# Row softmax on one core: row maxima moved to a general path, five large tiles in place of ten, late loads between two loops

## The chip, the cores and the metric

One core of a Trainium2 chip. The time is the device's, in microseconds (us), from one execution; the "span" of a profile, from its first to its last instruction, is 1.3 to 1.4 us shorter. On this one core "slow" means a run over 1.5% above the fastest of its kernel.

## The reference, cut to what matters

```python
x: (16, 1024, 512) float32
x_scaled = x / 2.0
exp_x = np.exp(x_scaled - np.max(x_scaled, axis=-1, keepdims=True))
return exp_x / np.sum(exp_x, axis=-1, keepdims=True)
```

There are 16384 rows of 512 numbers. On the chip they lie as 128 partitions by 128 rows; "a row" below is one row on all 128 partitions: 0.262 MB. All data are read once and written once, 67.1 MB in all.

## The kernel before

It keeps 98 rows on chip (the arena). Ten tiles of 3 to 15 rows are loaded, worked on in place and stored; the last two reuse the places of the first four. VectorE finds row maxima, ScalarE computes exp with its row sum, VectorE divides. SyncE issues the stores, ScalarE nearly all loads.

```python
PLAN = [
    ([3], 0), ([4, 3], 3), ([5, 4, 4], 10), ([5] * 3, 23), ([5] * 3, 38), ([5] * 3, 53),
    ([5] * 3, 68), ([5] * 3, 83), ([5] * 3, 0), ([5] * 3, 15),
]                                        # rows of each chunk of a tile, place in the arena
LAG = 2
...
    def do_max(k):
        nc.vector.reduce_max(out=stats[:, b : b + c], in_=arena[:, a : a + c], negate=True, ...
        )._wait_ge(ld[t], ...).then_inc(s_max, 1)
...
        for k in range(len(chunks) + LAG):
            if k < len(chunks):
                do_max(k)
            if k >= LAG:
                do_mul(k - LAG)          # reciprocal of the sums, then the product
...
                ins = nc.scalar.activation(
                    out=arena[:, a + r], in_=arena[:, a + r], func=Exp, scale=0.5,
                    bias=stats[:, b + r : b + r + 1], accum_out=stats[:, b + r : b + r + 1],
                )
...
        for t in range(len(tiles)):      # SyncE
            nc.sync.wait_ge(s_mul, last_chunk[t] + 1)
            nc.sync.dma_start(out=dram(of, t), in_=sb(t)).then_inc(...)
```

Of the kernel before, what the change touches and what calls it, by code (L numbers as in the profile page):

```python
# [6 lines left out]




PLAN = [
    ([3], 0), ([4, 3], 3), ([5, 4, 4], 10), ([5] * 3, 23), ([5] * 3, 38), ([5] * 3, 53),
    ([5] * 3, 68), ([5] * 3, 83), ([5] * 3, 0), ([5] * 3, 15),
]
ARENA = 98
LAG = 2

SPREAD = 1

AFTER = {8: 4, 9: 5}  # L20

FUSED = {1, 2, 3}

LOOP = 6
E = 5


@with_exitstack
def kernel(
# [5 lines left out]
    nc = tc.nc  # L35
    tc.close()
    tc.compile()
    fp32 = mybir.dt.float32

    xf = x.flatten_outer_dims()  # L40
    of = out.flatten_outer_dims()
    N, D = xf.shape
    P = nc.NUM_PARTITIONS
    n_rows = N // P
    assert sum(sum(c) for c, _ in PLAN) == n_rows

    arena = nc.alloc_sbuf_tensor("arena", (P, ARENA, D), fp32)

    stats = nc.alloc_sbuf_tensor("stats", (P, n_rows), fp32)
    recip = nc.alloc_sbuf_tensor("recip", (P, n_rows), fp32)  # L50



    tiles, chunks, base = [], [], 0
    for t, (cs, at) in enumerate(PLAN):
        r = sum(cs)
        tiles.append((base, r, at))
        o = 0
        for c in cs:
            chunks.append((t, base + o, c, at + o))  # L60
            o += c
        base += r
    last_chunk = {c[0]: k for k, c in enumerate(chunks)}

    def dram(ap, t):
        b, r, _ = tiles[t]
        return ap[b * P : (b + r) * P].rearrange("(p r) d -> p r d", r=r)

    def sb(t):
        _, r, at = tiles[t]  # L70
        return arena[:, at : at + r, :]


    behind = {}
    for t, (_, r, at) in enumerate(tiles):
        for u in range(t):
            _, ru, au = tiles[u]
            if at < au + ru and au < at + r:
                behind.setdefault(t, []).append(u)

    ld = [nc.alloc_semaphore(f"ld{t}") for t in range(len(tiles))]
    awaited = sorted({u for us in behind.values() for u in us})


    st, need = {}, {}
    for t in sorted(behind):
        new = [u for u in behind[t] if u not in st]
        sem = nc.alloc_semaphore(f"st{t}")
        st.update({u: sem for u in new})
        need[t] = (sem, 16 * len(new))  # L90
    s_end = nc.alloc_semaphore("s_end")
    s_max = nc.alloc_semaphore("s_max")
    s_exp = nc.alloc_semaphore("s_exp")
    s_go = nc.alloc_semaphore("s_go")
    s_rec = nc.alloc_semaphore("s_rec")
    s_mul = nc.alloc_semaphore("s_mul")

    def issue_loads(begin, end):


        for t in range(begin, end):
            if t in behind:
                continue
            if t == 0:
                nc.sync.dma_start(out=sb(t), in_=dram(xf, t)).then_inc(ld[t], 16)
            elif t == SPREAD:

                r = tiles[t][1] - 1
                for p, q, lo, hi in ((0, P, 0, r), (0, 126, r, r + 1), (126, P, r, r + 1)):
                    nc.scalar.dma_start(  # L110
                        out=sb(t)[p:q, lo:hi], in_=dram(xf, t)[p:q, lo:hi]
                    ).then_inc(ld[t], 16)
            else:
                nc.scalar.dma_start(out=sb(t), in_=dram(xf, t)).then_inc(ld[t], 16)

    def do_max(k):
        t, b, c, a = chunks[k]
        nc.vector.reduce_max(  # L118
            out=stats[:, b : b + c],
            in_=arena[:, a : a + c],  # L120
            axis=mybir.AxisListType.X,
            negate=True,
        )._wait_ge(ld[t], 48 if t == SPREAD else 16).then_inc(s_max, 1)

    def do_mul(k):
        t, b, c, a = chunks[k]
        nc.vector.reciprocal(  # L127
            out=recip[:, b : b + c], in_=stats[:, b : b + c]
        )._wait_ge(s_exp, k + 1).then_inc(s_rec, 1)
        if t in FUSED:  # L130
            nc.vector.tensor_mul(  # L131
                out=arena[:, a : a + c],
                in0=arena[:, a : a + c],
                in1=recip[:, b : b + c].unsqueeze(2).to_broadcast([P, c, D]),
            )._wait_ge(s_rec, k + 1).then_inc(s_mul, 1)
            return
        for r in range(c):
            ins = nc.vector.tensor_scalar_mul(  # L138
                out=arena[:, a + r],
                in0=arena[:, a + r],  # L140
                scalar1=recip[:, b + r : b + r + 1],
            )
            if r == 0:
                ins._wait_ge(s_rec, k + 1)
        ins.then_inc(s_mul, 1)

    def compute_and_store():

        for k in range(len(chunks) + LAG):
            if k < len(chunks):  # L150
                do_max(k)
            if k >= LAG:
                do_mul(k - LAG)


        for t in range(len(tiles)):
            nc.sync.wait_ge(s_mul, last_chunk[t] + 1)
            nc.sync.dma_start(out=dram(of, t), in_=sb(t)).then_inc(
                st[t] if t in awaited else s_end, 16
            )  # L160

        nc.sync.wait_ge(s_end, 16 * (len(tiles) - len(awaited)))


        straight = [k for k, c in enumerate(chunks) if c[0] < LOOP]
        loop = [k for k, c in enumerate(chunks) if c[0] >= LOOP]
        for k in loop:
            nc.tensor.wait_ge(s_max, k + 1).then_inc(s_go, 1)


        nc.scalar.preload_act_table(mybir.ActivationFunctionType.Exp)  # L171
        late = sorted(behind)
        for k in straight:
            t, b, c, a = chunks[k]
            for r in range(c):
                ins = nc.scalar.activation(  # L176
                    out=arena[:, a + r],
                    in_=arena[:, a + r],
                    func=mybir.ActivationFunctionType.Exp,
                    bias=stats[:, b + r : b + r + 1],  # L180
                    scale=0.5,
                    accum_out=stats[:, b + r : b + r + 1],
                )
                if r == 0:
                    ins._wait_ge(s_max, k + 1)
            ins.then_inc(s_exp, 1)
            while late and last_chunk[AFTER[late[0]]] <= k:
                u = late.pop(0)
                nc.scalar.wait_ge(*need[u])
                nc.scalar.dma_start(out=sb(u), in_=dram(xf, u)).then_inc(ld[u], 16)  # L190
        assert not late


        first = chunks[loop[0]][1]
        assert all(
            c == E and b == first + j * E and a == b % ARENA
            for j, (_, b, c, a) in enumerate(chunks[k] for k in loop)
        )
        row = nc.scalar.alloc_register("row")
        nc.scalar.reg_mov(row, first)  # L200
        with nc.scalar.While(lambda: nc.scalar.snap(row, min_val=first, max_val=n_rows) < n_rows):
            now = nc.scalar.snap(row, min_val=first, max_val=n_rows - E)
            nc.scalar.wait_ge(s_go, 1).then_inc(s_go, -1)  # L203
            at = nc.s_assert_within(
                now % ARENA, 0, ARENA - E,
                skip_runtime_bounds_check_because="no chunk reaches over the arena's end",
            )
            for r in range(E):
                data = arena[:, r : ARENA - E + 1 + r][:, bass.ds(at, 1)]
                stat = stats[:, r : n_rows - E + 1 + r][:, bass.ds(now, 1)]  # L210
                ins = nc.scalar.activation(  # L211
                    out=data,
                    in_=data,
                    func=mybir.ActivationFunctionType.Exp,
                    bias=stat,
                    scale=0.5,
                    accum_out=stat,
                )
            ins.then_inc(s_exp, 1)
            nc.scalar.reg_add(row, row, E)  # L220



    here = str(nc.cur_bb)
    entry, rest = nc.main_func.blocks[0], list(nc.main_func.blocks[1:])
    head, jumps = entry.instructions[:-5], entry.instructions[-5:]
    entry.instructions = []
    nc.switch_bb("main", None)
    issue_loads(0, 2)
    first = list(entry.instructions)  # L230
    at = next(k for k, i in enumerate(head) if type(i).__name__ == "InstDrain")
    entry.instructions = head[:at] + first + head[at:]
    act = []
    entry.instructions = list(entry.instructions) + [i for i in jumps if i not in act]
    nc.switch_body(here, parent=None, valid_engines=[i.engine for i in jumps])
    issue_loads(2, len(tiles))
    compute_and_store()


# [28 lines left out]
```

## Time and profile before

| | before |
|---|---|
| time | 160.08 us, median of 3 |
| span of the profile | 158.6 us |
| VectorE busy | 131.4 us |
| ScalarE busy | 94.4 us |
| bytes over the span | 67.1 MB, 423 GB/s |

The prediction shows the lines of the profile. In them DVE is VectorE, ACT ScalarE, PE TensorE, POOL GpSimd and SP SyncE; a q after a name is the queue on which that engine issues, and L132 is a line of the kernel. Two things to keep in mind when reading them: the DMA row says in how many tenths of each slice the 16 DMA engines moved something, and it is full nearly everywhere; and a row of idle time on VectorE or ScalarE costs nothing while that is so.

### The profile page before, as it was taken

What the parts mean: (1) busy time and instruction counts of PE and PEld (TensorE: products, weight loads), DVE (VectorE), ACT (ScalarE), POOL (GpSimd) and SP (SyncE); (2) the same over time, 40 slices, a digit from 0 to 9 for tenths busy, and PEclk for the clock granted to TensorE, in tenths of its full rate; (3) what the DMA queues carried; (4) which work ended last, traced back from release to release, by engine and by line L of the source; (5) the groups of instructions that cost most, each with busy time, mean ns of one, the idle gap of its engine ahead of it and who ended that gap; (6) DMA issues with size and microseconds to landing.
All of it is one profiled execution on the core that took longest, in us unless ns stands there. A gap on an engine that the chain in (4) does not pass through costs nothing.

```text
span 158.6 us, 621 instructions
## 1 busy us (share of the span) xinstructions
DVE 131.4 (83%) x155; ACT 94.4 (60%) x257; POOL 0.2 (0%) x4
## 2 busy tenths in 40 slices
DVE  0466799999999999999999999996999389999000
ACT  0369197736874594669738797666566809763000
POOL 0000000000000000000000000000000000000000
DMA  7999999999999999999999999999999999999996
GB/s 268 449 373 430 414 431 466 435 407 399 466 443 389 434 463 448 418 444 426 442 426 434 426 426 442 426 441 411 457 395 472 395 473 395 472 395 465 395 472 263
DMA packets 3026, 67.13 MB, mean 423 GB/s; under 512 B 336, under 2 KB 336, under 8 KB 720
## 3 DMA queue, kind: packets, MB, share of 16 engines
q1 hardware_dynamic: 1584, 34.34, 50.6%
q10 hardware_dynamic: 1440, 32.77, 48.5%
q14 instruction: 2, 0.02, 0.0%
HBM read 33.55 MB, written 33.55 MB: 423 GB/s over the span
## 4 chain that ended last, share of the span: by engine, by line
DMA 52%; DVE 38%; issue 0%
DMA arena<-in_x_dram 38%; DVE stats L118 18%; DMA out_dram<-arena 14%; DVE arena L131 13%; DVE arena L138 7%; DVE recip L127 1%
## 5 line engine op out<-in xcount | busy, mean ns | idle before, releaser
L118 DVE TENSOR_REDUCE stats<-arena 128x5 f32<-128x2560 f32 (+2 forms) x27 | 72.2, 2676 | 14.6 <-DMA arena<-in_x_dram 14.6
L176 ACT ACTIVATE arena<-arena,stats 128x512 f32<-128x512 f32 x68 | 48.2, 710 | 23.4 <-DVE stats L118 23.4
L211 ACT ACTIVATE arena<-arena,stats x60 | 42.5, 710 | 20.7 <-ACTq L203 20.7
L138 DVE TENSOR_SCALAR arena<-arena,recip 128x512 f32<-128x512 f32 x93 | 38.6, 482 | 0.7
L131 DVE TENSOR_TENSOR arena<-arena,recip 128x2560 f32<-128x2560 f32 (+2 forms) x8 | 19.9, 2491 | 0.3
L176 ACT ACTIVATION_READ_ACCUMULATOR arena<-arena,stats 128x1 f32 x68 | 12.7, 187 | 0.0
L211 ACT ACTIVATION_READ_ACCUMULATOR arena<-arena,stats x60 | 11.2, 187 | 0.0
L127 DVE RECIPROCAL recip<-stats 128x5 f32<-128x5 f32 (+2 forms) x27 | 4.8, 177 | 0.0
L171 ACT ACT_TABLE_LOAD x1 | 1.3, 1283 | 5.7 <-issue 5.7
L252 POOL MEMSET const-bfloat16-1.0<- 128x1 bf16 x1 | 0.1, 101 | 0.0
L252 POOL MEMSET const-uint8-127<- 128x1 uint8 x1 | 0.1, 101 | 0.0
L252 POOL MEMSET const-float32-0.0<- 128x1 f32 x1 | 0.1, 98 | 0.2 <-issue 0.2
L252 POOL MEMSET const-float32-1.0<- 128x1 f32 x1 | 0.1, 98 | 0.0
## 6 DMA issues: line engine op xcount, KB each, us to landing
arena<-in_x_dram ACTq DMA_DIRECT2D x7, 3840.0 KB, 46.6
out_dram<-arena SPq DMA_DIRECT2D x7, 3840.0 KB, 22.7
arena<-in_x_dram ACTq DMA_DIRECT2D x1, 3328.0 KB, 14.3
out_dram<-arena SPq DMA_DIRECT2D x1, 3328.0 KB, 21.1
out_dram<-arena SPq DMA_DIRECT2D x1, 1792.0 KB, 18.2
arena<-in_x_dram ACTq DMA_DIRECT2D x1, 1536.0 KB
arena<-in_x_dram SPq DMA_DIRECT2D x1, 768.0 KB, 6.2
out_dram<-arena SPq DMA_DIRECT2D x1, 768.0 KB, 15.8
```

The lines of the kernel that those rows point to most:

```text
L118: nc.vector.reduce_max(out=stats[:, b : b + c], in_=arena[:, a : a + c], axis=mybir.AxisListType.X, negate=True,)._wait_ge(ld[t], 48 if t ...
L127: nc.vector.reciprocal(out=recip[:, b : b + c], in_=stats[:, b : b + c])._wait_ge(s_exp, k + 1).then_inc(s_rec, 1)
L131: nc.vector.tensor_mul(out=arena[:, a : a + c], in0=arena[:, a : a + c], in1=recip[:, b : b + c].unsqueeze(2).to_broadcast([P, c, D]),)._w ...
L138: ins = nc.vector.tensor_scalar_mul(out=arena[:, a + r], in0=arena[:, a + r], scalar1=recip[:, b + r : b + r + 1],)
L171: nc.scalar.preload_act_table(mybir.ActivationFunctionType.Exp)
L176: ins = nc.scalar.activation(out=arena[:, a + r], in_=arena[:, a + r], func=mybir.ActivationFunctionType.Exp, bias=stats[:, b + r : b + r ...
L211: ins = nc.scalar.activation(out=data, in_=data, func=mybir.ActivationFunctionType.Exp, bias=stat, scale=0.5, accum_out=stat,)
L252: nc = _bacc.Bacc("TRN2", target_bir_lowering=False, num_devices=1)
```

## The change

The intent: VectorE, the busiest engine, is freed of the row maxima. exp(x/2) is taken without subtracting anything; at the end the kernel counts the row sums that lie between 1 and 1e30, and only if one doesn't, a general path computes everything again with maxima. The ten tiles become five. Two loads that reuse the arena are issued by ScalarE between two loops, after row 70.

```diff
-PLAN = [ ([3], 0), ([4, 3], 3), ([5, 4, 4], 10), ([5] * 3, 23), ... ]
+TILES = [(30, 8), (30, 38), (30, 68), (25, 0), (13, 25)]     # rows, place
+TURN = 70
...
-                do_max(k)
...
-                    bias=stats[:, b + r : b + r + 1],
...
+    def early():
+        load(nc.sync, 0)
+    def loads():
+        load(nc.scalar, 1)
+        load(nc.scalar, 2)
...
+        exponentials(0, TURN)
+        nc.scalar.wait_ge(s_first, 16)        # store of tile 0 has landed
+        load(nc.scalar, 3)
+        load(nc.scalar, 4)
+        exponentials(TURN, n_rows - LAST)
...
+        nc.vector.tensor_scalar(out=inside, in0=stats, scalar1=LO, scalar2=HI, op0=max, op1=min)
+        ... is_equal, reduce_sum, a 1x1 matmul, flag
+        rounds(nc.vector, vector); rounds(nc.scalar, scalar); rounds(nc.sync, sync)   # general path
```

(Shortened; cut are semaphores, asserts and the general path's body. All 26 products are now one tensor_mul per chunk of five rows, three in the last.)

More of the change, by code (lines that the diff above doesn't have):

```diff
@@ L6 @@
 from concourse._compat import with_exitstack
-PLAN = [
-    ([3], 0), ([4, 3], 3), ([5, 4, 4], 10), ([5] * 3, 23), ([5] * 3, 38), ([5] * 3, 53),
-    ([5] * 3, 68), ([5] * 3, 83), ([5] * 3, 0), ([5] * 3, 15),
-]
+TILES = [(30, 8), (30, 38), (30, 68), (25, 0), (13, 25)]
 ARENA = 98
-LAG = 2
-SPREAD = 1
-AFTER = {8: 4, 9: 5}
-FUSED = {1, 2, 3}
-LOOP = 6
+SHIFT = 8
 E = 5
+LAST = 3
+TURN = 70
+LO, HI = 1.0, 1.0e30
+G = 8
 @with_exitstack
@@ L38 @@
     fp32 = mybir.dt.float32
+    Exp = mybir.ActivationFunctionType.Exp
+    Alu = mybir.AluOpType
     xf = x.flatten_outer_dims()
@@ L44 @@
     n_rows = N // P
-    assert sum(sum(c) for c, _ in PLAN) == n_rows
+    assert sum(r for r, _ in TILES) == n_rows
     arena = nc.alloc_sbuf_tensor("arena", (P, ARENA, D), fp32)
@@ L50 @@
     recip = nc.alloc_sbuf_tensor("recip", (P, n_rows), fp32)
-    tiles, chunks, base = [], [], 0
-    for t, (cs, at) in enumerate(PLAN):
-        r = sum(cs)
+    inside = nc.alloc_sbuf_tensor("inside", (P, n_rows), fp32)
+    count = nc.alloc_sbuf_tensor("count", (P, 1), fp32)
+    ones = nc.alloc_sbuf_tensor("ones", (P, 1), fp32)
+    flag = nc.alloc_sbuf_tensor("flag", (1, 1), mybir.dt.int32)
+    g_max = nc.alloc_sbuf_tensor("g_max", (P, G), fp32)
+    g_sum = nc.alloc_sbuf_tensor("g_sum", (P, G), fp32)
+    total = nc.alloc_psum_tensor("total", (1, 1), fp32)
+    tiles, base = [], 0
+    for r, at in TILES:
+        assert at == (base + SHIFT) % ARENA
         tiles.append((base, r, at))
-        o = 0
-        for c in cs:
-            chunks.append((t, base + o, c, at + o))
-            o += c
         base += r
-    last_chunk = {c[0]: k for k, c in enumerate(chunks)}
     def dram(ap, t):
@@ L71, in sb @@
         return arena[:, at : at + r, :]
-    behind = {}
-    for t, (_, r, at) in enumerate(tiles):
-        for u in range(t):
-            _, ru, au = tiles[u]
-            if at < au + ru and au < at + r:
-                behind.setdefault(t, []).append(u)
-    ld = [nc.alloc_semaphore(f"ld{t}") for t in range(len(tiles))]
-    awaited = sorted({u for us in behind.values() for u in us})
-    st, need = {}, {}
-    for t in sorted(behind):
-        new = [u for u in behind[t] if u not in st]
-        sem = nc.alloc_semaphore(f"st{t}")
-        st.update({u: sem for u in new})
-        need[t] = (sem, 16 * len(new))
+    starts = list(range(0, n_rows - LAST, E)) + [n_rows - LAST]
+    sizes = [E] * (len(starts) - 1) + [LAST]
+    assert n_rows - LAST == E * (len(starts) - 1)
+    owner = [max(t for t, (b, _, _) in enumerate(tiles) if b <= s) for s in starts]
+    assert all(s + c <= sum(tiles[t][:2]) for s, c, t in zip(starts, sizes, owner))
+    upto = [1 + max(k for k, o in enumerate(owner) if o == t) for t in range(len(tiles))]
+    ld = [nc.alloc_semaphore(f"ld{t}") for t in range(len(tiles))]
+    s_first = nc.alloc_semaphore("s_first")
     s_end = nc.alloc_semaphore("s_end")
-    s_max = nc.alloc_semaphore("s_max")
     s_exp = nc.alloc_semaphore("s_exp")
@@ L96 @@
     s_mul = nc.alloc_semaphore("s_mul")
-    def issue_loads(begin, end):
-        for t in range(begin, end):
-            if t in behind:
-                continue
-            if t == 0:
-                nc.sync.dma_start(out=sb(t), in_=dram(xf, t)).then_inc(ld[t], 16)
-            elif t == SPREAD:
-                r = tiles[t][1] - 1
-                for p, q, lo, hi in ((0, P, 0, r), (0, 126, r, r + 1), (126, P, r, r + 1)):
-                    nc.scalar.dma_start(
-                        out=sb(t)[p:q, lo:hi], in_=dram(xf, t)[p:q, lo:hi]
-                    ).then_inc(ld[t], 16)
-            else:
-                nc.scalar.dma_start(out=sb(t), in_=dram(xf, t)).then_inc(ld[t], 16)
@@ L116, in do_max @@
-    def do_max(k):
-        t, b, c, a = chunks[k]
-        nc.vector.reduce_max(
-            out=stats[:, b : b + c],
-            in_=arena[:, a : a + c],
-            axis=mybir.AxisListType.X,
-            negate=True,
-        )._wait_ge(ld[t], 48 if t == SPREAD else 16).then_inc(s_max, 1)
-    def do_mul(k):
-        t, b, c, a = chunks[k]
-        nc.vector.reciprocal(
-            out=recip[:, b : b + c], in_=stats[:, b : b + c]
-        )._wait_ge(s_exp, k + 1).then_inc(s_rec, 1)
-        if t in FUSED:
+    s_ones = nc.alloc_semaphore("s_ones")
@@ new lines, with load, store @@
+    s_cnt = nc.alloc_semaphore("s_cnt")
+    s_tot = nc.alloc_semaphore("s_tot")
+    s_flag = nc.alloc_semaphore("s_flag")
+    g_ld = nc.alloc_semaphore("g_ld")
+    g_st = nc.alloc_semaphore("g_st")
+    g_neg = nc.alloc_semaphore("g_neg")
+    g_exp = nc.alloc_semaphore("g_exp")
+    g_rec = nc.alloc_semaphore("g_rec")
+    g_mul = nc.alloc_semaphore("g_mul")
+    def load(eng, t):
+        eng.dma_start(out=sb(t), in_=dram(xf, t)).then_inc(ld[t], 16)
+    def store(t):
+        nc.sync.wait_ge(s_mul, upto[t])
+        nc.sync.dma_start(out=dram(of, t), in_=sb(t)).then_inc(
+            s_first if t == 0 else s_end, 16
+        )
@@ new lines, in take, with rounds @@
+    def take(eng, sem, n):
+        eng.wait_ge(sem, n).then_inc(sem, -n)
+    def rounds(eng, body):
+        last = n_rows // G
+        i = eng.alloc_register("tile")
+        eng.wait_ge(s_flag, 1)
+        eng.reg_load(i, flag[0:1, 0:1])
+        with eng.While(lambda: eng.snap(i, min_val=0, max_val=last) < last):
+            body(eng.snap(i, min_val=0, max_val=last - 1))
+            eng.reg_add(i, i, 1)
+    def early():
[3 more added lines that the diff above has]
+        load(nc.scalar, 2)
@@ L131, in do_mul, with program @@
+    def program():
+        nc.vector.memset(ones[:, :], 1.0).then_inc(s_ones, 1)
+        for k, (b, c) in enumerate(zip(starts, sizes)):
+            a = (b + SHIFT) % ARENA
+            nc.vector.reciprocal(
+                out=recip[:, b : b + c], in_=stats[:, b : b + c]
+            )._wait_ge(s_exp, k + 1).then_inc(s_rec, 1)
             nc.vector.tensor_mul(
@@ L135, in do_mul @@
             )._wait_ge(s_rec, k + 1).then_inc(s_mul, 1)
-            return
-        for r in range(c):
-            ins = nc.vector.tensor_scalar_mul(
-                out=arena[:, a + r],
-                in0=arena[:, a + r],
-                scalar1=recip[:, b + r : b + r + 1],
-            )
-            if r == 0:
-                ins._wait_ge(s_rec, k + 1)
-        ins.then_inc(s_mul, 1)
-    def compute_and_store():
-        for k in range(len(chunks) + LAG):
-            if k < len(chunks):
-                do_max(k)
-            if k >= LAG:
-                do_mul(k - LAG)
-        for t in range(len(tiles)):
-            nc.sync.wait_ge(s_mul, last_chunk[t] + 1)
-            nc.sync.dma_start(out=dram(of, t), in_=sb(t)).then_inc(
-                st[t] if t in awaited else s_end, 16
-            )
-        nc.sync.wait_ge(s_end, 16 * (len(tiles) - len(awaited)))
-        straight = [k for k, c in enumerate(chunks) if c[0] < LOOP]
-        loop = [k for k, c in enumerate(chunks) if c[0] >= LOOP]
-        for k in loop:
-            nc.tensor.wait_ge(s_max, k + 1).then_inc(s_go, 1)
-        nc.scalar.preload_act_table(mybir.ActivationFunctionType.Exp)
-        late = sorted(behind)
-        for k in straight:
-            t, b, c, a = chunks[k]
-            for r in range(c):
-                ins = nc.scalar.activation(
-                    out=arena[:, a + r],
-                    in_=arena[:, a + r],
-                    func=mybir.ActivationFunctionType.Exp,
-                    bias=stats[:, b + r : b + r + 1],
-                    scale=0.5,
-                    accum_out=stats[:, b + r : b + r + 1],
-                )
-                if r == 0:
-                    ins._wait_ge(s_max, k + 1)
-            ins.then_inc(s_exp, 1)
-            while late and last_chunk[AFTER[late[0]]] <= k:
-                u = late.pop(0)
-                nc.scalar.wait_ge(*need[u])
-                nc.scalar.dma_start(out=sb(u), in_=dram(xf, u)).then_inc(ld[u], 16)
-        assert not late
-        first = chunks[loop[0]][1]
-        assert all(
-            c == E and b == first + j * E and a == b % ARENA
-            for j, (_, b, c, a) in enumerate(chunks[k] for k in loop)
-        )
-        row = nc.scalar.alloc_register("row")
@@ new lines, in program @@
+        nc.vector.tensor_scalar(
+            out=inside[:, :], in0=stats[:, :], scalar1=LO, scalar2=HI,
+            op0=Alu.max, op1=Alu.min,
+        ).then_inc(s_cnt, 1)
+        nc.vector.tensor_tensor(
+            out=inside[:, :], in0=inside[:, :], in1=stats[:, :], op=Alu.is_equal
+        )._wait_ge(s_cnt, 1).then_inc(s_cnt, 1)
+        nc.vector.reduce_sum(
+            out=count[:, :], in_=inside[:, :], axis=mybir.AxisListType.X
+        )._wait_ge(s_cnt, 2).then_inc(s_cnt, 1)
+        nc.vector.tensor_scalar(
+            out=flag[:, :], in0=total[:, :], scalar1=float(N), scalar2=float(n_rows // G),
+            op0=Alu.is_ge, op1=Alu.mult,
+        )._wait_ge(s_tot, 1).then_inc(s_flag, 1)
@@ new lines, in program @@
+        for t in range(len(tiles)):
+            nc.tensor.wait_ge(ld[t], 16).then_inc(s_go, owner.count(t))
+        nc.tensor.wait_ge(s_ones, 1)
+        nc.tensor.matmul(
+            total[:, :], lhsT=count[:, :], rhs=ones[:, :], start=True, stop=True
+        )._wait_ge(s_cnt, 3).then_inc(s_tot, 1)
+        nc.scalar.preload_act_table(Exp)
+        exponentials(0, TURN)
[3 more added lines that the diff above has]
+        exponentials(TURN, n_rows - LAST)
@@ new lines, in program @@
+        take(nc.scalar, s_go, 1)
+        for b in range(n_rows - LAST, n_rows):
+            a = (b + SHIFT) % ARENA
+            ins = nc.scalar.activation(
+                out=arena[:, a], in_=arena[:, a], func=Exp, scale=0.5,
+                accum_out=stats[:, b : b + 1],
+            )
+        ins.then_inc(s_exp, 1)
+        for t in range(len(tiles)):
+            store(t)
+        x_g = xf.rearrange("(t p r) d -> t p r d", p=P, r=G)
+        o_g = of.rearrange("(t p r) d -> t p r d", p=P, r=G)
@@ new lines, in program, with vector @@
+        data = arena[:, 0:G]
+        def vector(i):
+            take(nc.vector, g_ld, 16)
+            nc.vector.reduce_max(
+                out=g_max[:, :], in_=data, axis=mybir.AxisListType.X, negate=True
+            ).then_inc(g_rec, 1)
+            take(nc.vector, g_rec, 1)
+            nc.vector.tensor_scalar_mul(
+                out=g_max[:, :], in0=g_max[:, :], scalar1=0.5
+            ).then_inc(g_neg, 1)
+            take(nc.vector, g_exp, 1)
+            nc.vector.reciprocal(out=g_sum[:, :], in_=g_sum[:, :]).then_inc(g_rec, 1)
+            take(nc.vector, g_rec, 1)
+            nc.vector.tensor_mul(
+                out=data, in0=data, in1=g_sum[:, :].unsqueeze(2).to_broadcast([P, G, D])
+            ).then_inc(g_mul, 1)
@@ new lines, in scalar, with sync @@
+        def scalar(i):
+            take(nc.scalar, g_neg, 1)
+            for r in range(G):
+                ins = nc.scalar.activation(
+                    out=arena[:, r], in_=arena[:, r], func=Exp, scale=0.5,
+                    bias=g_max[:, r : r + 1], accum_out=g_sum[:, r : r + 1],
+                )
+            ins.then_inc(g_exp, 1)
+        def sync(i):
+            nc.sync.wait_ge(s_end, 16 * (len(tiles) - 1))
+            nc.sync.dma_start(
+                out=data, in_=x_g[bass.ds(i, 1)].rearrange("o p r d -> (o p) r d")
+            ).then_inc(g_ld, 16)
+            take(nc.sync, g_mul, 1)
+            nc.sync.dma_start(
+                out=o_g[bass.ds(i, 1)].rearrange("o p r d -> (o p) r d"), in_=data
+            ).then_inc(g_st, 16)
+            take(nc.sync, g_st, 16)
@@ L200, in compute_and_store, with exponentials @@
+        rounds(nc.vector, vector)
+        rounds(nc.scalar, scalar)
+        rounds(nc.sync, sync)
+        nc.sync.wait_ge(s_end, 16 * (len(tiles) - 1))
+    def exponentials(first, end):
+        row = nc.scalar.alloc_register(f"row{first}")
         nc.scalar.reg_mov(row, first)
-        with nc.scalar.While(lambda: nc.scalar.snap(row, min_val=first, max_val=n_rows) < n_rows):
-            now = nc.scalar.snap(row, min_val=first, max_val=n_rows - E)
-            nc.scalar.wait_ge(s_go, 1).then_inc(s_go, -1)
+        with nc.scalar.While(lambda: nc.scalar.snap(row, min_val=first, max_val=end) < end):
+            now = nc.scalar.snap(row, min_val=first, max_val=end - E)
+            take(nc.scalar, s_go, 1)
@@ L204, in compute_and_store @@
             at = nc.s_assert_within(
-                now % ARENA, 0, ARENA - E,
+                (now + SHIFT) % ARENA, 0, ARENA - E,
                 skip_runtime_bounds_check_because="no chunk reaches over the arena's end",
@@ L209, in compute_and_store @@
                 data = arena[:, r : ARENA - E + 1 + r][:, bass.ds(at, 1)]
-                stat = stats[:, r : n_rows - E + 1 + r][:, bass.ds(now, 1)]
                 ins = nc.scalar.activation(
-                    out=data,
-                    in_=data,
-                    func=mybir.ActivationFunctionType.Exp,
-                    bias=stat,
-                    scale=0.5,
-                    accum_out=stat,
+                    out=data, in_=data, func=Exp, scale=0.5,
+                    accum_out=stats[:, r : n_rows - E + 1 + r][:, bass.ds(now, 1)],
                 )
@@ L228 @@
     nc.switch_bb("main", None)
-    issue_loads(0, 2)
+    early()
     first = list(entry.instructions)
@@ L235 @@
     nc.switch_body(here, parent=None, valid_engines=[i.engine for i in jumps])
-    issue_loads(2, len(tiles))
-    compute_and_store()
+    loads()
+    program()
 _INS = ['x']
```

## The prediction

> **What bounds the kernel now.** I read the page first, then the windows by stage, the sizes and landings of the DMAs, the chain of waits, and the timeline of ScalarE and VectorE around the loop. The page's busy lines:
>
> ```profile
> DVE 131.4 (83%) x155; ACT 94.4 (60%) x257; POOL 0.2 (0%) x4
> DMA  7999999999999999999999999999999999999996
> HBM read 33.55 MB, written 33.55 MB: 423 GB/s over the span
> ```
>
> The 16 DMA engines are full in every slice but the first and the last. VectorE is busy 83%, but it waits for nothing the DMA would not also have to do. The windows (stretch; length and busy times; clock, DMA share, GB/s) give the rate by stage:
>
> ```profile
> 0.00:2.00 2.00, 0.00 (x0) 0.00 (x0) 0.20 (x4) 1.00 0.48 126
> 2.00:6.20 4.20, 0.00 (x0) 0.46 (x1) 0.00 (x0) 1.00 1.04 423
> 9.27:17.00 7.73, 5.32 (x7) 6.01 (x18) 0.00 (x0) 1.00 0.98 422
> 59.00:82.00 23.00, 22.82 (x32) 15.04 (x42) 0.00 (x0) 1.00 1.01 437
> 82.00:109.00 27.00, 25.90 (x39) 20.96 (x58) 0.00 (x0) 1.00 1.01 434
> 127.60:147.00 19.40, 19.11 (x33) 10.91 (x30) 0.00 (x0) 1.00 1.00 431
> 147.00:158.60 11.60, 0.00 (x0) 0.00 (x0) 0.00 (x0) 1.00 0.88 381
> ```
>
> 126 GB/s over the first 2 us is 0.25 MB, so data flow from about 1.4 us. One row (128 partitions x 2 KB) is 0.262 MB. At 0.432 MB/us, the mean of the middle, a row takes 0.607 us, and 256 row moves (128 in, 128 out) take 155.4. [...] The measured time is 160.08, so 1.5 us lie outside the span. The kernel is at the floor of its DMA traffic: a changed kernel that moves the same bytes can only lose, by idle DMA, or win by a better rate.
>
> How the two queues share the engines shows in the issues (size, us from issue to landing):
>
> ```profile
> out_dram<-arena SPq DMA_DIRECT2D x7, 3840.0 KB, 22.7
> out_dram<-arena SPq DMA_DIRECT2D x1, 3328.0 KB, 21.1
> out_dram<-arena SPq DMA_DIRECT2D x1, 1792.0 KB, 18.2
> out_dram<-arena SPq DMA_DIRECT2D x1, 768.0 KB, 15.8
> ```
>
> Tiny stores take nearly as long as large ones. Each partition's contiguous run is one packet (queue q1 counts 1584 = 11 DMAs x 144), so each engine has 8 data packets of a DMA. If a store packet of n rows alternates with a load packet of 15 rows, 8 pairs take 8 x (n+15) x 0.0759 us (0.607/8): 10.9, 13.4, 17.0, 18.2 for 3, 7, 13, 15 rows. Measured less that: 4.9, 4.8, 4.1, 4.5, a constant of 4.5. [...] So the share goes by packet, not by need.
>
> ScalarE's rows:
>
> ```profile
> L176 ACT ACTIVATE arena<-arena,stats 128x512 f32<-128x512 f32 x68 | 48.2, 710 | 23.4 <-DVE stats L118 23.4
> L211 ACT ACTIVATION_READ_ACCUMULATOR arena<-arena,stats x60 | 11.2, 187 | 0.0
> 86.51 0.72 ACT L211 ACTIVATE arena<-arena,stats  x1 [0.49 <-ACTq L203]
> 87.23 0.71 ACT L211 ACTIVATE arena<-arena,stats  x1
> 87.94 0.71 ACT L211 ACTIVATE arena<-arena,stats  x1
> ```
>
> A row costs 0.705 us start to start: 710 + 187 less two overlaps of 96 ns. In the loop and in straight code it is the same, so the register work between two rows is hidden.
>
> [...] the load at 62.88 us was issued by ScalarE's sequencer while the activations of the chunk ahead of it ran until 65.1.
>
> **The change, part by part.**
> Row maxima. 27 TENSOR_REDUCE, 72.2 us of VectorE, go. VectorE keeps per chunk of five a reciprocal (0.1 net) and a multiply of 2.83, about 3.0; 26 chunks are 77 us. None of that was on the DMA's path: worth 0 directly.
>
> Bias. Without maxima the activation's bias is an immediate zero. [...] The loop's branch and register work runs ahead of the engine: from a maximum's end to the next activation was 0.36 us, including TensorE's relay[...]. Hence 3.06 per chunk, 78 us for 128 rows.
>
> Tiles. The first tile was 3 rows, landed at 6.2 us, and stores began at 14.65. Now it is 30 rows on SyncE's queue, and ScalarE's queue brings tiles 1 and 2 from about 4.2 us (issue at 2.65 as before, plus the delay). A packet is now 30 rows, 2.28 us per engine. Tile 0 takes its 8 packets; two or three go alone, the others alternate with tile 1: 13 to 14 packets, 1.4 + 14 x 2.28 = 33.3[...]. I take 34. All 90 rows are in at 1.4 + 54.6 = 56.0.
>
> First store. ScalarE starts at 34.4, ends six chunks at 52.8, VectorE ends the sixth 3.1 later, at 55.9: store 0 moves data from 57.3 to 75.5. Gap in the DMA: **1.3**. Reads alone ran at 418 GB/s in the first 17 us, against 432 later; if that is a matter of reading, 65 more rows read alone cost 17.04 MB x (1/0.418 - 1/0.432) = 1.3, and fill the gap. So 1.3 either way.
>
> Store 1 is ready at 34.4 + 12 x 3.06 + 3.1 = 74.2 and follows with no gap over 0.1.
>
> Loads between the loops. Store 0 lands at 77.0. Row 70 is done at 34.4 + 14 x 3.06 = 77.2: the turn fits, ScalarE loses under 1 us. Loads 3 and 4 move from about 78.7.
>
> The mixed stage. Store 1 has 25 rows left and alternates 30 against 25 with load 3: 25 x 55/30 x 0.607 = 28, until 106.5, load 3 having 21. Its last 4 against store 2 take 5.6: it lands near 113.5. ScalarE has been idle since 90; this costs nothing, as the DMA is full. Tile 3 is computed by 129 and multiplied by 132, before store 2 ends near 134, so store 3 follows without a gap. Load 4 (13-row packets against 30) lands at about 139. Tile 4 takes 2 x 3.06 + 3 x 0.61 = 8.0 on ScalarE and 2.1 on VectorE, so store 4 is issued at 149.6 and moves from 151. Store 3 ends at about 150: **1.0** lost.
>
> The check of the sums. Three small VectorE operations, one 1x1 matmul, a flag and three register loads, all after the last multiply, while store 4 moves 13 rows for 7.9 us: hidden. The general path is not entered: sums of 512 terms exp(x/2) of normal x lie in the hundreds.
>
> Sum: 158.6 + 1.3 + 0.1 + 1.0 = 161.0 of span, plus 1.5: 162.5. I shade it to 162.2, since tile 0 may land a little earlier.
>
> **Rivals.** (a) ScalarE becomes the bound in the first 80 us, because the sequencer can't hide the loop: a chunk of 3.5 us instead of 3.06. Then store 0 starts 2.6 later, store 1 leaves a gap of nearly 3, and a further 1.8 opens before store 3: about 168. For it: no iteration of the old loop had its chunk waiting, so the loop's own cost was never seen bare. Against it: the 0.36 us, and the equal pitch. (b) Tile 0 lands late, at 36 to 38, because its packets take strict turns from the start: gap of 3 to 5 at the first store, and 164 to 166. (c) Larger packets raise the rate, or the early read stage turns out no slower: with no gap at all the floor is 158.5 + 1.5, about 160. The full engines speak against anything below that. (d) The gain of a lighter VectorE shows in the time: the idle rows of VectorE speak against it, since the DMA never waited.
>
> **Range and chances.** Nothing can gain more than a fraction of a per cent without a better rate: faster by 2% (under 156.9) gets 0.03. The middle, with gaps of 0 to 3, is within 2% (to 163.3): 0.64. Rivals (a) and (b), or both in part, give 0.33 for slower. 160.0 to 166.0 should hold it 8 times in 10.
>
> **What would show it.** The first landing of a 30-row load at 33 to 36; [...]pitch 0.61, and no idle between chunks while data are there; VectorE about 77 us; a dip in the DMA row near 56 us, one in the last tenth, and none between; a long idle of ScalarE, about 90 to 113, ended by load 3. A dip at 74 to 80 or chunks over 3.2 would show rival (a); a landing after 36, rival (b). A time under 160 would mean the rate rose, and my floor was wrong.

The whole came to 161.0 of span and 162.5 of time, shaded to 162.2; none of its terms (158.6, 1.3, 0.1, 1.0 and 1.5) is cut, but terms of the sums under them are. The 3.06 us of a chunk, on which the 1.3 and the 1.0 rest, are five rows at a pitch of 0.612 us; the changed kernel then showed 613 ns for an activation, 0.61 us from row to row and 3.06 us from chunk to chunk. The 34 us for tile 0 were 33.3 and an allowance for the landing; 37.3 was measured. That larger packets bring no better rate was an assumption; 433 GB/s was measured against 431 to 437.

## The result, and the profile after

The changed kernel took **167.16 us** (median of 4 runs, 165.66 to 168.59; one of the four counts as slow) against 160.06 before. The ratio of the fast runs is **1.041** (1.033 to 1.049). Ratios here and below are the mean time of one kernel's fast runs over that of the other's in the same rounds, so not quite the ratio of the medians. The general path was not entered and the result is correct. The prediction was 162.2 with a range to 166.0: the time is outside.

The profiled run is the slowest of the fast ones, 167.65 us. Its page, in the order of the lines shown of before:

```profile
PE 0.2 (0%) x2; PEld 0.1 (0%) x2; DVE 78.1 (47%) x57; ACT 80.1 (48%) x257; POOL 0.2 (0%) x4
DMA  7999988999988487999989999999898999999893
HBM read 33.55 MB, written 33.55 MB: 403 GB/s over the span
```

VectorE lost 53 us of work and ScalarE 14, as predicted, and the span grew by 7.7 us. The DMA row has what it didn't have before: a dip around the 14th slice (54 to 58 us) and a thin end.

The DMA issues of the changed kernel (size, us from issue to landing):

```profile
arena<-in_x_dram SPq DMA_DIRECT2D x1, 7680.0 KB, 37.0
out_dram<-arena SPq DMA_DIRECT2D x1, 3328.0 KB, 11.3
```

Tile 0 was issued at 0.25 us, so it landed at 37.3, and the first exponential follows at once:

```profile
37.60 0.63 ACT L237 ACTIVATE arena<-arena  x1 [33.66 <-ACTq L104]
38.23 0.61 ACT L237 ACTIVATE arena<-arena  x1
38.84 0.61 ACT L237 ACTIVATE arena<-arena  x1
```

The windows of the changed kernel (stretch; length; busy time of PE, PEld, DVE, ACT and POOL with counts; clock, DMA share, GB/s):

```profile
5.00:55.00 50.00, 0.00 (x0) 0.00 (x0) 13.99 (x10) 17.40 (x57) 0.00 (x0) 1.00 1.00 433
55.00:60.50 5.50, 0.00 (x0) 0.00 (x0) 5.41 (x5) 5.50 (x19) 0.00 (x0) 1.00 0.45 190
60.50:79.00 18.50, 0.00 (x0) 0.00 (x0) 18.21 (x13) 18.50 (x61) 0.00 (x0) 1.00 0.99 425
79.00:92.00 13.00, 0.00 (x0) 0.00 (x0) 12.18 (x9) 12.48 (x41) 0.00 (x0) 1.00 0.94 353
92.00:140.00 48.00, 0.00 (x0) 0.00 (x0) 19.55 (x13) 16.86 (x56) 0.00 (x0) 1.00 1.00 422
```

The first store:

```profile
59.18 0.34 SPq L99 DMA_DIRECT2D out_dram<-arena  x1
```

Three readings. Reading alone (5 to 55) runs at 433 GB/s, as fast as the 431 to 437 of the kernel before. From 55 to 60.5 the engines move at 190: the reads have ended and the first store, issued at 59.18, is not there yet (its first packets start at 60.0). And from 79 to 92, when loads 3 and 4 join the stores, the share is nearly full but only 353 GB/s come of it, where the kernel before has 444 in the same stretch:

```profile
79.00:92.00 13.00, 12.89 (x18) 8.80 (x25) 0.00 (x0) 1.00 1.03 444
```

The trace also keeps a record of each packet, with start, duration and size. From these I worked out two sums for every kernel, each an average over the 16 engines: **idle**, the time with no packet in flight, and **stretch**, what packets took beyond their size over 27.1 bytes per ns (a 30-row packet of 61,440 bytes takes 2.267 us where nothing disturbs it, a 15-row one 1.138; each contiguous run is one record, 1440 for the ten DMAs of the changed kernel, 144 each, 128 of data and 16 of completion). 67.1 MB at that rate take 154.8 us; with idle and stretch they give each span to within 0.4 us. A record does not name its engine; where engines are told apart, each packet was put behind the one that had just ended, which gives 16 chains. The sums:

```
                    span   idle  stretch   time (median)
before             158.6    1.7    2.4      160.08
changed            166.3    7.2    4.3      167.16   (this profile 167.65)
 of the idle: 1.6 at the start, 3.4 from 55 to 62, 0.5 from 62 to 160, 1.8 at the end
```

So of the 7.7 us, 5.5 are idle engines and 1.9 are slow packets. The experiments ask why.

### The profile page after: what moved, and what is told of

Read it like the earlier page. It is cut to its first block, busy times and chain, and to the rows that moved or that the text cites. A ratio compares the mean times of both kernels' runs of the same rounds, so it can differ in the third digit from the quotient of the medians.

```text
span 166.3 us, 680 instructions
## 1 busy us (share of the span) xinstructions
PE 0.2 (0%) x2; PEld 0.1 (0%) x2; DVE 78.1 (47%) x57; ACT 80.1 (48%) x257; POOL 0.2 (0%) x4
## 5 line engine op out<-in xcount | busy, mean ns | idle before, releaser
L237 ACT ACTIVATE arena<-arena x125 | 76.6, 613 | 69.1 <-ACTq L104 69.1
L132 DVE TENSOR_TENSOR arena<-arena,recip 128x2560 f32<-128x2560 f32 (+1 forms) x26 | 72.4, 2784 | 0.9
L129 DVE RECIPROCAL recip<-stats 128x5 f32<-128x5 f32 (+1 forms) x26 | 4.9, 189 | 75.0 <-ACT arena L237 74.8
L237 ACT ACTIVATION_READ_ACCUMULATOR arena<-arena x125 | 23.3, 186 | 0.0
L169 ACT ACTIVATE arena<-arena 128x512 f32<-128x512 f32 x3 | 1.8, 612 | 0.0
L169 ACT ACTIVATION_READ_ACCUMULATOR arena<-arena 128x1 f32 x3 | 0.6, 186 | 0.0
```

The source lines that it names most:

```text
L129: nc.vector.reciprocal(out=recip[:, b : b + c], in_=stats[:, b : b + c])._wait_ge(s_exp, k + 1).then_inc(s_rec, 1)
L132: nc.vector.tensor_mul(out=arena[:, a : a + c], in0=arena[:, a : a + c], in1=recip[:, b : b + c].unsqueeze(2).to_broadcast([P, c, D]),)._w ...
L169: ins = nc.scalar.activation(out=arena[:, a], in_=arena[:, a], func=Exp, scale=0.5, accum_out=stats[:, b : b + 1],)
L237: ins = nc.scalar.activation(out=data, in_=data, func=Exp, scale=0.5, accum_out=stats[:, r : n_rows - E + 1 + r][:, bass.ds(now, 1)],)
```

## The experiments

The theory after the result: **(A)** the DMA sets the end, and the first 30-row tile lands so late that the engines run dry before the first store. **(C)** Packets of 30 rows make each of these losses larger: a completion waits for a packet of the other queue, and the engines finish further apart. Rivals: the loss is in the mixed stage after 80 us alone (B), the order of tiles and not the packet's size (D), or VectorE's load matters after all (rival B of run 1 alone). The letters are those of the expectations; from E on they are explained there. Ten runs were made. All gave correct results.

**1. The kernel before without its maxima.** One part of the change alone.

```diff
-            if k < len(chunks):
-                do_max(k)
...
-                    bias=stats[:, b + r : b + r + 1],
...
-                    ins._wait_ge(s_max, k + 1)
+                    ins._wait_ge(ld[t], 48 if t == SPREAD else 16)
```

> The kernel before without its row maxima and bias, everything else (tiles, queues, loop) as it was. Theory A (the DMA sets the end; VectorE's maxima cost nothing): 159.5 to 160.5 us, ratio 0.997 to 1.003, although VectorE loses 72 us of work and an activation falls from 710 to about 613 ns. Rival B (VectorE's load holds up the stores): under 158 us.

Measured: 160.12 us, ratio 1.0001 (0.998 to 1.002). Its page:

```profile
DVE 63.3 (40%) x128; ACT 80.7 (51%) x257; POOL 0.2 (0%) x4
DMA  7999999989899999999999999999999999999996
```

68 us of VectorE are gone and the DMA row is as full as it was, but for two slices at 8. Theory A: the maxima were worth nothing in the old tiles, because the chain of stores never waited for VectorE long enough to leave an engine without packets.

**2. The changed kernel with tile 0 alone on the engines.** Loads 1 and 2 go behind load 0 on the same queue.

```diff
-        load(nc.scalar, 1)
-        load(nc.scalar, 2)
+        load(nc.sync, 1)
+        load(nc.sync, 2)
```

> The changed kernel with loads 1 and 2 on SyncE's queue behind load 0, so that tile 0 has the engines to itself. Theory A (late first tile leaves the DMA idle for 3.4 us before the first store, and everything after it is that much later): tile 0 lands at about 20 us, store 0 is issued at about 42 and moves as soon as the reads end near 57, the dip there vanishes, 163.0 to 164.5 us. Rival B (the time is lost in the mixed stage after 80 us alone): the dip vanishes but the time stays at 166 to 168, since the later stages stretch.

Measured: 162.28 us (161.35 to 162.81), ratio 1.013. Tile 0 landed at 21.3, store 0, the first of the five stores merged in the first line below, was issued at 43.2, and the dip went (same windows):

```profile
43.23 108.11 SPq L99 DMA_DIRECT2D out_dram<-arena  x5
55.00:60.50 5.50, 0.00 (x0) 0.00 (x0) 5.40 (x5) 5.21 (x17) 0.00 (x0) 1.00 0.83 357
79.00:92.00 13.00, 0.00 (x0) 0.00 (x0) 10.01 (x8) 11.96 (x40) 0.00 (x0) 1.00 0.96 416
```

(By the packet records no engine is idle from 55 to 62 here. A window counts a packet whole where it starts, so a short one fluctuates by some packets, and its share can pass 1.) Rival B falls. But the time is below the range I wrote for theory A: not 3.4 at most but some 4.2 us came back (162.2 against 166.4, the mean of the changed kernel's seven fast runs in all). By the packet records, the stretch after 80 us went as well: 0.03 us from 80 to 95 instead of 1.7. In its place 0.9 lie at 54 us, where the stores take over from the reads. Every profile shows such a stall once, most of them about when loads and stores first overlap (the kernel before and run 1 some 10 to 20 us after their first store), and here it costs less than in the changed kernel. So this run does not separate the dip from the stall: both went, and only the dip was foreseen.

**3. The changed kernel with halved packets.** Every transfer is two transfers of half the rows, same queues, same order.

```diff
-        eng.dma_start(out=sb(t), in_=dram(xf, t)).then_inc(ld[t], 16)
+        for lo, hi in halves(t):
+            eng.dma_start(out=sb(t)[:, lo:hi], in_=dram(xf, t)[:, lo:hi]).then_inc(ld[t], 16)
```

(The stores alike, and the waits count 32.)

> The changed kernel with each of its ten transfers cut into two halves by rows, on the same queues in the same order, so packets are 15 rows at most in place of 30. Theory C (large packets cost: a completion waits for one packet of the other queue, engines finish further apart, packets stretch when a second queue starts): tile 0 lands at 35.5 to 36.3 instead of 37.3, the last DMAs end closer together, 163.5 to 165.5 us. Rival D (packet size doesn't matter, only the order of the tiles): 166 to 168.

Measured: 164.42 us (164.39 to 164.60), ratio 1.027: theory C, not D. One detail was a miss: tile 0's last engine landed at 37.3 as before, though the median engine came 1.0 us earlier. Idle fell from 7.2 to 5.5 and stretch from 4.3 to 3.4. The dip is still there, since only the packets changed:

```profile
55.00:60.50 5.50, 0.00 (x0) 0.00 (x0) 5.41 (x5) 5.50 (x19) 0.00 (x0) 1.00 0.43 184
79.00:92.00 13.00, 0.00 (x0) 0.00 (x0) 9.49 (x7) 9.75 (x33) 0.00 (x0) 1.00 1.00 396
```

What went is the thin end: the idle after 160 us fell from 1.8 to 0.5. The four runs lie within 0.2 us, where the changed kernel's fast ones lie within 2.

**4. Only loads 1 and 2 in halves.** Tile 0 keeps 30-row packets and now meets 15-row packets.

```diff
+        if t in (1, 2):
+            for lo, hi in ((0, 15), (15, 30)):
+                eng.dma_start(out=sb(t)[:, lo:hi], in_=dram(xf, t)[:, lo:hi]).then_inc(ld[t], 16)
+            return
```

> The changed kernel with only loads 1 and 2 cut into 15-row halves, load 0 left at 30-row packets. Theory A with sharing by packet: tile 0 gets two thirds of the engines, its data end near 27 and it lands at 28 to 29.5 us; store 0 is issued near 51, before the reads end, and the dip near 57 vanishes: 162.5 to 164.5 us. Rival E (sharing by bytes): tile 0 lands at 36 to 37.5 as before, and the time stays at 166 to 168.

Measured: 161.54 us (161.27 to 161.76), ratio 1.009. Sharing by packet, and not by bytes, is shown: tile 0 landed at 29.4 and store 0 was issued at 51.26, before the reads ended. The time is a miss: it lies below the range I wrote for theory A. As in run 2 more came back than the dip, some 4.9 us (161.5 against 166.4), since the stall after 80 us went too and left 1.0 us at 52 to 56 in its place. The issue line of tile 0 answers for the sharing by packet (37.0 us in the changed kernel):

```profile
arena<-in_x_dram SPq DMA_DIRECT2D x1, 7680.0 KB, 29.1
```

With runs 2 and 4 the landing can be taken apart. Each DMA ends, on each engine, with a packet of 4 bytes, and an increment of the semaphore follows it: in the changed kernel tile 0's 16 start at 35.7 to 36.9 us, and its 16 increments come at 36.1 to 37.3. On the median engine, from the packet records:

```
                       other queue's   tile 0's data   completion      wait
                       packets         end at          packet starts
changed kernel         30 rows         33.98           36.24           2.26
the same, run 5        30 rows         33.96           36.22           2.26
loads 1, 2 in halves   15 rows         27.21           28.34           1.13
all on one queue       none            20.50           20.50           0.00
```

The completion takes a turn of its own: it waits for exactly one packet of the other queue. This is the 2.3 us that my 14 packets lacked.

**5. The changed kernel again.**

> The changed kernel unaltered, for the noise and for the stalls in the mixed stage. Theory A (late landing of tile 0, systematic): tile 0 lands at 37.0 to 37.6 and the dip near 57 is 3.2 to 3.6 us of idle DMA again. Theory F (the rest of the loss is stalls and unequal engines in the mixed stage, different each time): the stretched packets and the spread at the end differ from the first profile by half a microsecond or more; 165.5 to 168.5 us, wider than any other version.

Measured: 166.29 us (165.80 to 168.82; the fast ones to 166.74), ratio 1.038; the profile fell on the slow run. Tile 0 landed at 37.1 and the gap was 3.3 us: systematic, theory A. Beyond it the two profiles differ, as theory F says; but this one is of the slow run. Load 4 ended on its engines between 140.0 and 143.3 us in the first, and between 140.5 and 146.4 in this one, with 14 of 16 engines done by 141.7. A load counts as landed when its slowest engine is done (in the first profile the 16 increments of load 4 came from 140.0 to 143.3, and its first activation started at 143.75), so store 4 was issued at 158.0 instead of 155.0, and 2.4 us of idle opened before it. This says what made this slow run slow. Of the fast runs only the first was profiled, so the cause of their spread (165.66 to 167.65) is not shown.

**6. The late loads later.** `TURN = 85` instead of 70.

> The changed kernel with the loads of tiles 3 and 4 between the loops at row 85 instead of 70, so some 9 us later. Theory G (the place of the loads is not where the time is lost as long as stores fill the DMA; but load 3 is later, tile 3 is computed later and the stores run dry): no idle DMA near 80, load 3 lands at 122 to 126, an idle stretch of 3 to 5 us before store 3 near 140: 169 to 173 us. Rival H (mixing loads with stores near 80 is what stretches the packets, and a later start helps): under 166.

Measured: 171.55 us, ratio 1.072: theory G, and H (under 166) falls. Load 3 landed at 126.1, as expected; the idle stretch is longer than the 3 to 5 us I wrote. The idle time shows where stores run dry (138 to 146 us, same columns):

```profile
138.00:146.00 8.00, 0.00 (x0) 0.00 (x0) 7.61 (x7) 7.86 (x27) 0.00 (x0) 1.00 0.39 166
```

By the packet records 6.3 us of idle lie between 138 and 152. The stall came with the loads, to 89.8 us, so it belongs to their start and not to a time. Row 70 is not too late: in the changed kernel store 0 landed at 78.81 and the load, which waits for it, was issued at 78.83.

**7. The maxima put back into the new tiles.** The other half of run 1: everything of the change but its removal of the maxima.

```diff
+            nc.vector.reduce_max(out=stats[:, b : b + c], in_=arena[:, a : a + c], negate=True, ...
+            )._wait_ge(ld[owner[k]], 16).then_inc(s_max, 1)
```

(with the bias of the kernel before, and TensorE passing on s_max per chunk)

> The changed kernel's five tiles and queues with the row maxima put back on VectorE (one TENSOR_REDUCE per chunk and the bias of the kernel before). Theory I (the large tiles lean on the quick compute: with VectorE at 5.7 us per chunk instead of 3.06 the DMA starves at the first store and at each later one): store 0 issued near 72 instead of 59, 185 to 200 us. Rival J (as in the old tiles, where the maxima cost nothing: the DMA has slack for them): 166 to 170 us.

Measured: 197.54 us, ratio 1.238: theory I, not J. Store 0 was issued at 71.56. Its DMA row has holes where the engines wait for VectorE:

```profile
PE 0.2 (0%) x2; PEld 0.1 (0%) x2; DVE 145.9 (74%) x83; ACT 93.3 (48%) x257; POOL 0.2 (0%) x4
DMA  9999999999940049994004999999899999099996
```

So the maxima cost 0 us in tiles of 3 to 15 rows and about 31 in tiles of 30. Removing them doesn't pay for itself; it only pays for part of what the large tiles cost. (The two are not quite the same experiment: the products here are the changed kernel's, 2.83 us a chunk, where most of the kernel before's are five operations that take 2.07, so VectorE has 145.9 us of work against 131.4.)

**8. A version meant to win: 15-row tiles, no maxima.** Eight tiles of 15 rows and one of 8, loads in order on ScalarE's queue, wrapped loads between three loops.

```diff
-TILES = [(30, 8), (30, 38), (30, 68), (25, 0), (13, 25)]
+TILES = [(15, 8), (15, 23), (15, 38), (15, 53), (15, 68), (15, 83), (15, 0), (15, 15), (8, 30)]
-TURN = 70
+TURN, TURN2 = 45, 60
```

> A version for both ends: no row maxima, but eight tiles of 15 rows and one of 8, all loads in order on ScalarE's queue, the wrapped ones between three loops at rows 45 and 60. Theory A (the DMA sets the end; what counts is that it never runs dry and that its first packets aren't small): tile 0 lands at 10.5 to 11.5, store 0 is issued near 24, no idle DMA between start and end, 157.8 to 159.3 us, under the kernel before. Rival K (the floor of the kernel before is the floor of this traffic): 159.8 to 160.5.

Measured: 160.87 us (160.35 to 161.54), ratio 1.004: a miss, above the ranges of both A and K. Idle 2.8 (1.3 of it in the last 5 us, by engines that end at different times) and stretch 3.0 (1.3 when the first store meets the loads near 27 us).

**9. Both cures on the changed kernel.** Runs 2 and 3 together.

> The changed kernel with both cures at once: loads 1 and 2 behind load 0 on SyncE's queue, and every transfer in two halves by rows. Theory L (late first tile and unequal engines under large packets are two separate losses and together make up the difference to the kernel before): no dip near 57, loads 3 and 4 landing within 2 us over the engines, no idle DMA before the last store, 160.2 to 161.3 us. Rival M (the same loss counted twice, so the second cure adds nothing to the first): 162 to 163, as with the queue alone.

Measured: 160.73 us (160.65 to 161.86), ratio 1.005: theory L, not M. By the means, 5.5 us came back, against 4.2 and 2.0 for the two cures alone. Its DMA row is that of the kernel before:

```profile
DMA  7999999999999999999999999999999999999996
```

Idle is 2.3 and stretch 2.7. Load 4 ends between 135.1 and 136.3 on its engines. The late first tile and the large packets together explain the loss, but for half a per cent. (The queue cure also moves the stall, so the two parts are not quite pure.)

**10. Run 8 with a small first tile** (5 and 10 rows in place of the first 15).

> The version of 15-row tiles with its first tile cut into 5 and 10 rows, so that stores begin earlier and in smaller packets. Theory N (the stall when loads and stores first meet is smaller with small packets, 0.4 us instead of 1.3, and the stores start near 12 us): 159.2 to 160.0 us, under the kernel before by up to half a per cent. Rival O (the stall is the same, or the loss is at the end, by unequal engines): 160.3 to 161.2.

Measured: 160.59 us, ratio 1.003 (1.001 to 1.004): rival O's range. The stall did shrink, to 0.5 us, as theory N said, but the time didn't follow. In the profiled run, the fastest of the five, idle is 2.1 and stretch 2.3, no better than 1.7 and 2.4 before. I found no version under the kernel before; whether there is one stays open.

## Why the prediction was wrong, point by point

- **What bounds the kernel, and what the maxima are worth.** Right: run 1 gives 0.0%.
- **ScalarE's pitch.** Right: 613 ns for an activation without the pointer, against 710 with it in the kernel before, 0.61 us from row to row, no gap between chunks in the first loop. The loop's branch and register work is hidden. Rival (a) falls.
- **When tile 0 lands: the step that failed.** "13 to 14 packets, 1.4 + 14 x 2.28 = 33.3", and "I take 34." The 14 packets are right: the data were in at 34.0, 0.7 after the 33.3, since the first packets were slow (0.7 us of stretch before 5 us). The landing was the mis-sized term: from 33.3 to the 34 there is only 0.7 us for it. It is 3.3: the completion's own turn behind a 30-row packet, 2.26, and 1.0 more until the increment of the last engine arrived. The last store of the kernel before, with no other queue at work, landed 0.4 us after its data (158.2 to 158.6). Landing, 2.6 more than the 0.7, and data, 0.7, are the 3.3 us by which tile 0 was late (37.3). For the four stores of the kernel before I had counted eight pairs of packets, which holds such a turn; for tile 0 I counted 14 packets and none. And the constant of 4.5 that I found there is not landing: 3.6 to 4.3 us of it lie between the issue and the first packet, on the median engine. Rival (b), with its landing at 36 to 38 and a gap of 3 to 5, is what came, for a reason other than the one I gave it.
- **The first gap.** Predicted 1.3, and 1.3 "either way", since slow reading would fill it. Measured 3.4. Reading alone isn't slow: 433 GB/s from 5 to 55. The 418 before came of small first packets and starts: 0.7 us of stretch lie between 5 and 20 us there, most of it in the first packets of the load at 8 us. (The 418 takes in a window that the prediction does not show, 402 GB/s from 6.2 to 9.27.)
- **The turn at row 70.** Right: ScalarE ended row 70 at 80.5 against 77.2 predicted, later by the 3.3 of tile 0. Its sequencer, ahead of it, issued load 3 as store 0 landed, at 78.8, and ScalarE lost 0.5 us.
- **The mixed stage.** No term stood for it, and that is the second failure. Load 3 landed at 120.1, not 113.5, load 4 at 143.3, not 139. I had load 3 move data from 78.7; issued at 78.83, it had its first packets at 83.8 to 86.3, 5.0 to 7.5 us later, on engines that the stores kept busy. This start, mis-sized by some 6 us, is about what load 3 was late by. It left hardly an engine idle (0.1 us from 80 to 140); what cost time is the rest. The stage cost 1.7 us of stalled packets at its start and ended with engines 3.3 us apart. I had treated 16 engines as one, and a window at 432 GB/s as true of every mixture.
- **The end.** Predicted: 1.0 idle before store 4 (the terms given, 139 + 8.0 + 2.1, make the issue 149.1 and not 149.6, so 0.5). Measured: 0.2 there, but 1.8 after it, because the engines do not finish together.
- **The check of the sums.** Right: 1.3 us on VectorE and TensorE after the last product at 154.9, under a store that ends at 166.3.

The sum of the terms, by the idle and stretch of both kernels: the first gap 2.1 more than predicted (3.4 against 1.3); idle from 62 us to the end 1.7 more than the kernel before, where 1.1 was predicted, so 0.6; the start 0.4 (1.6 against 1.2); stretch 1.9. That is 5.0 of the 5.3 us by which this profile's span of 166.3 exceeds the 161.0 predicted.

What stays open: why packets stall once in every profile. In the changed kernel the slow packets are first the store's, those that started at 80.8 to 83.1, before any packet of load 3, and then the first ones of load 3. The size by kernel: about 0.2 us in the kernel before (30 to 38 us), 0.4 in run 1 (22 to 28) and 0.5 in run 10 (13 to 17), where the first stores are 3 or 5 rows; 0.8 to 0.9 where the stores follow the reads on one queue (runs 2 and 9); 1.0 to 1.3 where they join 15-row loads (runs 4, 8); 1.1 with 15-row packets and 1.6 to 1.7 with 30-row packets where loads join running stores (run 3; runs 6, 7 and the changed kernel; 2.8 in the slow run 5). It fits the packet's size, but no run isolates it.

## What to carry to other kernels

When DMA sets the end, ask of each change only whether some engine is left without a packet: here 68 us less of VectorE bought nothing, and a first tile that landed late cost 3.4 us of idle engines (55 to 62 us) that nothing later recovered. Size the first tile and its neighbours on the other queue by packets: here it shared by turns (it landed at 37.3 us beside 30-row packets, at 29.4 beside 15-row ones, at 21.3 alone), waited one more turn for its completion (2.26 us, 1.13 and 0), and had landed when its slowest engine was done (37.3 us, where the median engine's completion started at 36.24). Count the wait for the first packet too, from issue, on the median engine: 0.9 to 1.2 us on idle engines, 3.6 to 4.3 for the stores of the kernel before among packets of up to 15 rows, 5.1 and 7.2 for loads 1 and 3 of the changed kernel among packets of 30. Large packets did not raise the rate (433 GB/s against 431) and made these waits longer: 2.26 us against 1.13 for a completion, and 3.3 us between the engines at the end of load 4 against 1.0 in run 3.
